# The opening of the first feed-forward: order of the first loads, scaling before squaring, and a norm factor computed with the tokens on partitions

## The chip, the core and the metric

The kernel runs on one core of a Trainium2 chip. The metric is the device time of one execution in microseconds (us), from the first to the last instruction of the program and what lies around it. Engines are named as in the profile: PE is TensorE, PEld its weight loads, DVE is VectorE, ACT is ScalarE, POOL is GpSimd and SP is SyncE, which here only issues DMAs.

## What is computed

One step of a decoder layer on 520 tokens: 512 of a new sequence and 8 of running sequences. The model width is 1024.

```
h = x
h = h + 0.5 * swiglu(rms_norm(h, ffn1_norm), gate1, up1, down1)      # 1024 -> 2816 -> 1024
h = h + mixer(rms_norm(h, mix_norm), ...)                            # pooling heads and SSD heads
h = h + 0.5 * swiglu(rms_norm(h, ffn2_norm), gate2, up2, down2)
y = rms_norm(h, final_norm)

rms_norm(x, g) = x * rsqrt(mean(x*x) + 1e-6) * g
swiglu(x)      = (silu(x @ gate) * (x @ up)) @ down
```

The change concerns the first line of this: the first norm and the first units of the first feed-forward. All values are float32.

## The kernel before

**Layout.** Features lie on the 128 partitions and tokens along the free axis, so `h` is 8 slices of 128 x 520, and every matmul has a 128 x 128 block of weights against 260 tokens, one of the two halves of the 520. A slice of `x` is written straight into `h`; its first slice comes with the vectors (norm gains and so on) in one DMA of 640 columns.

**Exact products from fast ones.** A matmul of plain float32 operands is two passes in the trace. Most products use three matmuls in the faster type fp32r instead (`mm3`): both operands are split into a rounded high part and a low part. `split` (L109 to L117) makes them for weights: ACT casts the high part (`whi`, `shi`), DVE or a POOL DMA that accumulates makes the low part (`wlo`, `slo`). `prep_pair` (L217) makes `xth` and `xtl` from the scaled input `xg` in the same way.

**The norm factor is applied late.** The kernel multiplies with `xg = x * gain` (`scaled`, L213), and the factor `r = 1/sqrt(mean + eps)` of each token is multiplied into the products when they leave PSUM (`plain_out`, L390 onwards). So `r` is not needed before the first unit is complete. `squares` (L163, L166) has ACT square the slices and DVE add them into `acc`. In `scales`, the 128 partitions of `acc` are summed by two matmuls with a matrix of ones (`psr_f`, L173), which leaves the sum of each token on all 128 partitions; ACT takes the root (L174, after a load of its function table) and DVE the reciprocal (L175) of 128 x 260 values, twice.

**The opening.** A unit is 128 of the 2816 hidden features, with a gate block and an up block. Unit 0 is multiplied in plain float32 while the input is still arriving (`plain`, L340): for each j of 0 to 3, slices j and j + 4 of `x` are loaded, then the two parts of the gate and up block (`raw`) that belong to them. The second unit, number 3, is partly plain (L360) and partly split (L369, `plain_mixed`, with `pwhi` and `pwlo` made by ACT and POOL). The third unit, number 1, is the first with the full split scheme (tiles `whi_1a`, `shi_1c`, `shi_1d`, `whi_1b` and their low parts).

**PSUM.** Eight banks in four tags of two. Tag `ps` serves, in turn, the sums of the norm (`psr`), and the up block of unit 3 (`P_310`, `P_311`). A third tile under that tag has to wait until the first has been read.

**Order.** A scheduler orders each engine's instructions at build time from its own estimate of their times. `tc.high_priority()` lets a block go ahead, and `tc.issue_after(i)` puts instructions of the same engine behind `i`. Each engine is given its instructions as one list and works it off in that order. SP issues all the loads of weights and input, in the written order; the eight loads in flight use eight semaphores in turn.

The second feed-forward has the other way of making the factor already, in `turned_scales` (L525): the sums are made with the tokens on 104 partitions, 5 groups of them (`turned`, L186: five matmuls with `acc` as weights and two columns of ones), so that root and reciprocal work on 104 x 10 values, and then five matmuls with an identity matrix `ident` (`spread`, L197) put the result on all 128 partitions again, in two PSUM tiles `pr_t` of tag `ps`, from which ACT copies it to `r` (L531).

Of the kernel before, what the change touches and what calls it, by code (L numbers as in the profile page):

```python
# [23 lines left out]
KD = D // P  # L24
# [38 lines left out]
def tile_trunk_step(ctx: ExitStack, tc: tile.TileContext, ins: dict, outs: dict):  # L63
    nc = tc.nc
# [23 lines left out]
    ident = cst.tile([P, P], F32, tag="ident", name="ident")  # L88
# [3 lines left out]
    def raw_pair(name, hp=None):  # L92
        hp, nb = (wp, 2) if hp is None else (hp, 1)
        return hp.tile([P, 2, 1024], F32, tag="raw", bufs=nb, name=f"raw_{name}")
# [66 lines left out]
    def squares(nx, wx, d, name, hp=("tg", 2)):  # L161
        if d == 0:
            nc.scalar.activation(out=nx[2], in_=h[:, d], func=AF.Square)  # L163
            return
        sq = wx.tile([P, 2, HB], F32, tag=hp[0], bufs=hp[1], name=f"sq_{name}_{d}").rearrange("p b t -> p (b t)")
        made = nc.scalar.activation(out=sq, in_=h[:, d], func=AF.Square)  # L166
        nc.vector.tensor_tensor(out=nx[2], in0=nx[2], in1=sq, op=ALU.add)
        return made.ins
# [39 lines left out]
    def home(gp, nb, name):  # L208
        return gp.tile([P, 4, HB], F32, tag="g", bufs=nb, name=name)

    def scaled(xg, norm, j):
        for d, out in ((j, xg[:, 0::3]), (j + KD // 2, xg[:, 1:3])):
            nc.scalar.activation(out=out, in_=h[:, d].rearrange("p (b t) -> p b t", b=2), func=AF.Copy,  # L213
                                 scale=v(norm, d))
        return xg

    def prep_pair(nx, xg, xd, j):  # L217
        xth, xtl, _, _ = nx
        nc.vector.tensor_tensor(out=xd[:, 0:2], in0=xg[:, 0::2], in1=xg[:, 3:4].to_broadcast([P, 2, HB]),
                                op=ALU.subtract)  # L220
        nc.vector.scalar_tensor_tensor(out=xd[:, 2], in0=xd[:, 1], scalar=-1.0, in1=xg[:, 0], op0=ALU.mult,
                                       op1=ALU.subtract)
        nc.vector.scalar_tensor_tensor(out=xd[:, 3], in0=xd[:, 2], scalar=-1.0, in1=xg[:, 1], op0=ALU.mult,
                                       op1=ALU.subtract)
        for s, t in ((xg[:, 0:3], slice(0, 3)), (xd, slice(3, 7))):
            nc.scalar.copy(xth[:, j, t], s)
            nc.vector.tensor_tensor(out=xtl[:, j, t], in0=s, in1=xth[:, j, t].bitcast(F32), op=ALU.subtract)

    class Ffn:
# [81 lines left out]
                low(go, slice(1, 3))  # L311
                low(xd, slice(3, 7))

        def plain_load(self, f, j=None):
            if f not in self.raw:
                self.raw[f] = raw_pair(f"{self.i}_{f}")
            src = ins[f"w{self.i}gu"]
            for u in range(2):
                if j is None:
                    nc.sync.dma_start(out=self.raw[f][:, u], in_=src[2 * f + u])  # L320
                    continue
                q = (t.rearrange("p (q c) -> p q c", q=2)[:, :, j * P : j * P + P]
                     for t in (self.raw[f][:, u], src[2 * f + u]))
                nc.sync.dma_start(out=next(q), in_=next(q))
# [349 lines left out]
    ffn1 = Ffn(nx1, 1, wx1, None, 2)  # L674
    xg1 = []
    second = ffn1.order[1]
    for j in range(KD // 2):
        for d in (j, j + KD // 2):
            q = slice(NVEC + d * NT if d else 0, NVEC + (d + 1) * NT)
            nc.sync.dma_start(out=vx[:, q], in_=ins["x"][:, q])  # L680
        ffn1.plain_load(0, j)
        xg1.append(scaled(home(xo, 8, f"xg_f1{j}"), "ffn1_norm", j))
        with tc.high_priority():
            for d in (j, j + KD // 2):
                last = squares(nx1, wx1, d, "f1", ("ac", 3) if j == KD // 2 - 1 else ("tg", 2))
        ffn1.plain(0, xg1[j], j)
        prep_pair(nx1, xg1[j], home(xo, 8, f"xd_f1{j}"), j)
# [1 line left out]
    third = ffn1.order[2]  # L689
    ffn1.early[third] = ffn1.fetch(f"1_{third}", ins["w1gu"][2 * third : 2 * third + 2], xo)  # L690
    with tc.high_priority():
        root = ffn1.scales()
    ffn1.add_early(third)
    with tc.issue_after(last):
        ffn1.plain_split(second, xo)
# [48 lines left out]

    ps[0] = tc.alloc_tile_pool(name="ppm", bufs=8, space=PSUM, reuse_waits="tile")
    mixer(tc, ins, outs, dict(locals()))
    f2["xg"].release()
    xa[0].release()
# [5 lines left out]
    with tc.high_priority():  # L754
        f2["ffn"].plain_free(0)
        root = f2["ffn"].turned_scales()
# [63 lines left out]
def mixer(tc, ins, outs, e):  # L820
    nc = tc.nc
# [8 lines left out]
    mp = pool("mx", "right")  # L830

    ident = e["ident"]
    nc.sync.dma_start(out=ident, in_=ins["ident"])
    tri = cst.tile([P, P], F32, tag="tri", name="tri")
    nc.sync.dma_start(out=tri, in_=ins["tri"])
    sel = cst.tile([48, NH], F32, tag="sel", name="sel")
# [575 lines left out]
```

## Time and profile before

| | |
|---|---|
| time, median of 3 runs | 966.94 us (966.36 to 967.24) |
| the profiled execution | 964.7 us, of which the span of the trace is 962.9 us |
| PE / DVE / ACT / POOL busy | 941.1 / 857.9 / 693.7 / 231.2 us |
| share of the chain that ended last | PE 80%, DVE 9%, DMA 4%, ACT 3% |
| granted TensorE clock, mean | 0.996 |

The profiled execution is 2.2 us under the median, and 1.8 us of it lie outside the trace's span. Times in the profile count from the span's start. The chain of waits is followed back from the last instruction, so a step that is not in it can move by some amount with no effect. Matmuls overlap: a row's duration covers the pipeline too, and the distance from start to start says what a matmul costs.

### The profile page before, as it was taken

What the parts mean: (1) busy time and instruction counts of PE and PEld (TensorE: products, weight loads), DVE (VectorE), ACT (ScalarE), POOL (GpSimd) and SP (SyncE); (2) the same over time, 40 slices, a digit from 0 to 9 for tenths busy, and PEclk for the clock granted to TensorE, in tenths of its full rate; (3) what the DMA queues carried; (4) which work ended last, traced back from release to release, by engine and by line L of the source; (5) the groups of instructions that cost most, each with busy time, mean ns of one, the idle gap of its engine ahead of it and who ended that gap; (6) DMA issues with size and microseconds to landing.
All of it is one profiled execution on the core that took longest, in us unless ns stands there. A gap on an engine that the chain in (4) does not pass through costs nothing.

```text
span 962.9 us, 20257 instructions
## 1 busy us (share of the span) xinstructions
PE 941.1 (98%) x7652; PEld 922.7 (96%) x7652; DVE 857.9 (89%) x1613; ACT 693.7 (72%) x1296; POOL 231.2 (24%) x341
## 2 busy tenths in 40 slices
PE   7999999999999999999999999999999999999995
PEld 6999999999999999999999999999999999999995
DVE  7999899989989698688999966899999999999976
ACT  8777677667776475586758556777788878887964
POOL 0111211221121000156523111022243324332500
PEclk9999999999999999999999999999999999999998
DMA  8575775675657343246698777457598769877832
GB/s 245 149 174 118 181 178 129 151 187 135 164 140 173 84 151 110 61 165 179 160 270 224 162 176 166 115 140 177 129 226 218 160 165 223 191 166 173 215 102 90
DMA packets 66611, 157.01 MB, mean 163 GB/s; under 512 B 9480, under 2 KB 22728, under 8 KB 66512
## 3 DMA queue, kind: packets, MB, share of 16 engines
q1 hardware_dynamic: 41040, 103.78, 34.3%
q0 software_dynamic: 25472, 51.92, 29.8%
q8 instruction: 60, 0.98, 0.4%
q14 instruction: 39, 0.32, 0.1%
HBM read 148.33 MB, written 7.34 MB: 162 GB/s over the span
## 4 chain that ended last, share of the span: by engine, by line
PE 80%; DVE 9%; DMA 4%; ACT 3%; issue 2%; POOL 2%; DVEq 0%; SPq 0%; ACTq 0%; POOLq 0%
PE A L130 8%; PE A L126 8%; PE A L129 8%; PE BE L130 6%; PE BE L129 6%; PE BE L126 6%; PE P L340 3%; PE wo L126 2%; PE wo L130 2%; PE wo L129 2%; PE A2d L129 2%; PE A2d L126 2%; PE A2d L130 2%; PE A1d L130 2%; PE A1d L129 2%
## 5 line engine op out<-in xcount | busy, mean ns | idle before, releaser
L482 ACT COPY ac<-A 128x260 f32<-128x260 f32 x123 | 45.4, 369 | 13.5 <-PE A L130 13.5
L425 DVE TENSOR_TENSOR s<-raw 128x1024 f32<-128x1024 f32 x41 | 50.0, 1220 | 3.4 <-DMA raw<-in_w1gu 2.5
L126 PE MATMUL wo<-catg,whi_wo 128*128 128x260 f32 x128 | 37.2, 291 | 0.0
L340 PE MATMUL P<-xg_f,raw 128*128 128x260 f32 x128 | 31.8, 400 | 5.5 <-ACT sq_f L166 5.5
L126 PE MATMUL inz<-xh_mx,whi_inz 128*128 128x260 f32 x128 | 36.7, 287 | 0.0
L130 PE MATMUL inz<-xh_mx,wlo_inz 128*128 128x260 f32 x128 | 36.3, 284 | 0.3 <-DMA wlo_inz<-in_w_in 0.3
L126 PE MATMUL inx<-xh_mx,whi_inx 128*128 128x260 f32 x128 | 36.4, 284 | 0.0
L130 PE MATMUL wo<-catg,wlo_wo 128*128 128x260 f32 x128 | 36.2, 283 | 0.0
L129 PE MATMUL inz<-xl_mx,whi_inz 128*128 128x260 f32 x128 | 36.1, 282 | 0.0
L130 PE MATMUL inx<-xh_mx,wlo_inx 128*128 128x260 f32 x128 | 36.1, 282 | 0.0
L129 PE MATMUL wo<-catg,whi_wo 128*128 128x260 f32 x128 | 36.1, 282 | 0.0
L129 PE MATMUL inx<-xl_mx,whi_inx 128*128 128x260 f32 x128 | 36.1, 282 | 0.0
L1091 POOL DMA_DIRECT2D out_nss<-hs x32 | 20.5, 640 | 59.9 <-DVE hs L1109 58.8
L340 PEld LDWEIGHTS P<-xg_f,raw 128*128 128x128 f32 x128 | 25.0, 200 | 9.3 <-ACT sq_f L166 5.5
L1222 DVE TENSOR_TENSOR h<-wo,h 128x260 f32<-128x260 f32 x48 | 19.4, 422 | 14.8 <-PE wo L130 14.8
L950 DVE SCALAR_TENSOR_TENSOR A<-U,h,A 128x544 f32<-128x544 f32 x36 | 28.1, 782 | 4.3 <-ACT A L948 4.0
L494 DVE TENSOR_TENSOR tg<-BE,ac 128x520 f32<-128x520 f32 x41 | 28.5, 695 | 2.2 <-PE BE L130 2.1
L504 DVE TENSOR_TENSOR tg<-tg,r_f 128x520 f32<-128x520 f32 x41 | 28.6, 698 | 1.5 <-ACT tg L502 1.2
L109 ACT CAST whi_wo<-raw_wo 128x1024 fp32r<-128x1024 f32 x12 | 12.6, 1047 | 22.7 <-issue 18.2
L502 ACT ACTIVATE tg<-tg 128x520 f32<-128x520 f32 x41 | 26.2, 639 | 3.5 <-DVE tg L501 3.5
L501 DVE TENSOR_TENSOR tg<-tg,r_f 128x520 f32<-128x520 f32 x41 | 28.5, 696 | 0.1
L426 DVE TENSOR_TENSOR s<-s,raw 128x512 f32<-128x512 f32 x41 | 28.2, 688 | 0.0
(1812 smaller groups left out, 4805.3 us busy)
## 6 DMA issues: line engine op xcount, KB each, us to landing
raw<-in_w2gu SPq DMA_DIRECT2D x44, 512.0 KB, 4.8
raw<-in_w1gu SPq DMA_DIRECT2D x42, 512.0 KB, 4.7
raw_1d<-in_w1d SPq DMA_DIRECT2D x24, 384.0 KB, 3.6
raw_2d<-in_w2d SPq DMA_DIRECT2D x24, 384.0 KB, 4.1
raw_wo<-in_w_out SPq DMA_DIRECT2D x12, 512.0 KB, 5.2
wlo_wo<-in_w_out POOLq DMA_DIRECT2D x12, 512.0 KB, 6.9
ab<-scr_acs SPq DMA_DIRECT2D x8, 512.0 KB, 5.5
raw_inz<-in_w_in SPq DMA_DIRECT2D x8, 512.0 KB, 4.4
```

The source lines that it names most:

```text
L126: first = nc.tensor.matmul(ps, whi, xhi, start=start, stop=False, **kw)
L129: nc.tensor.matmul(ps, whi, xlo, start=False, stop=False, **kw)
L130: nc.tensor.matmul(ps, wlo, xhi, start=False, stop=stop, **kw)
L340: nc.tensor.matmul(self.banks[f, u][b][:, :HB], ws(self.raw[f][:, u], j + 4 * q), xg[:, slot[q]], start=j == q == 0, stop=j == 3 and q == ...
L425: nc.vector.tensor_tensor(out=s1, in0=diag, in1=up0, op=ALU.add)
L426: nc.vector.tensor_tensor(out=s2[:, 0], in0=s1[:, 1], in1=raw[:, 0, :nb], op=ALU.add)
L482: nc.scalar.copy(keep, out[:, :HB])
L494: nc.vector.tensor_tensor(out=tg, in0=self.BE[k][:, :, :HB], in1=a, op=ALU.add)
L501: nc.vector.tensor_tensor(out=tg, in0=tg, in1=r, op=ALU.mult)
L502: nc.scalar.activation(out=tg, in_=tg, func=AF.Silu)
L504: nc.vector.tensor_tensor(out=tg, in0=tg, in1=r, op=ALU.mult)
L950: nc.vector.scalar_tensor_tensor(out=A[:, :n], in0=U[:, j : j + n], scalar=w(j), in1=A[:, :n], op0=ALU.mult, op1=ALU.add)
```

## The change

Three edits in the opening of the first feed-forward, and a DMA that moves with them.

1. `plain_load` takes the block (`u`) that it loads; the loop issues slice j, the gate part, slice j + 4, the up part, where it issued both slices first and then both parts.
2. For j = 0 the squares lose their high priority, so that the scaling of the slice (`scaled`) goes first.
3. `ffn1.scales()` becomes `ffn1.turned_scales()`. The value it returns, behind which the splits of the third unit are put by `issue_after(root)`, is now the reciprocal on DVE and no longer the root on ACT.
4. `ident`, which the new way needs, is loaded at j = 1 by SP, ahead of slices 2, 6, 3 and 7 of `x`; before it stood with the mixer's constants.

```
-        def plain_load(self, f, j=None):
+        def plain_load(self, f, j=None, us=(0, 1)):
...
-            for u in range(2):
+            for u in us:
...
     for j in range(KD // 2):
-        for d in (j, j + KD // 2):
+        for u, d in enumerate((j, j + KD // 2)):
             q = slice(NVEC + d * NT if d else 0, NVEC + (d + 1) * NT)
             nc.sync.dma_start(out=vx[:, q], in_=ins["x"][:, q])
-        ffn1.plain_load(0, j)
+            ffn1.plain_load(0, j, (u,))
+        if j == 1:
+            nc.sync.dma_start(out=ident, in_=ins["ident"])
         xg1.append(scaled(home(xo, 8, f"xg_f1{j}"), "ffn1_norm", j))
-        with tc.high_priority():
+        with tc.high_priority() if j else nullcontext():
             for d in (j, j + KD // 2):
                 last = squares(nx1, wx1, d, "f1", ("ac", 3) if j == KD // 2 - 1 else ("tg", 2))
...
     with tc.high_priority():
-        root = ffn1.scales()
+        root = ffn1.turned_scales()
     ffn1.add_early(third)
...
     with tc.issue_after(root):
         ffn1.open(third)
...
-    nc.sync.dma_start(out=ident, in_=ins["ident"])
```

What the scheduler makes of it, at three places. On SP, the first loads before (`h` is the input, `raw_0` the blocks of unit 0):

```order
L680 DMA h<-in_x 128x640
L680 DMA h<-in_x 128x520
L324 DMA raw_0_93<-in_w1gu 128x2x128 x2
L680 DMA h<-in_x 128x520 x2
L324 DMA raw_0_93<-in_w1gu 128x2x128 x2
```

and now:

```order
L680 DMA h<-in_x 128x640
L324 DMA raw_0_92<-in_w1gu 128x2x128
L680 DMA h<-in_x 128x520
L324 DMA raw_0_92<-in_w1gu 128x2x128
L680 DMA h<-in_x 128x520
L324 DMA raw_0_92<-in_w1gu 128x2x128
L680 DMA h<-in_x 128x520
L324 DMA raw_0_92<-in_w1gu 128x2x128
L683 DMA ident<-in_ident 128x128
```

The first gate part is now second in the queue and no longer third, and `ident` goes ahead of four slices of the input.

On ACT, from the last preparation of unit 3's weights (`pwlo_31`) to the root of the norm, before:

```order
L349 ACTIVATE pwlo_31_233<-raw_3_208 128x1024
L226 CAST xth_f_87<-xd_f_171 128x1040
L226 CAST xth_f_87<-xg_f_183 128x780
L226 CAST xth_f_87<-xd_f_200 128x1040
L174 ACT_TABLE_LOAD
L174 ACTIVATE r_f_90<-psr_f_214,eps 128x260
L174 ACTIVATE r_f_90<-psr_f_218,eps 128x260
L109 CAST whi_1a<-raw_1_211 128x1024
L113 ACTIVATE wlo_1a<-raw_1_211 128x512
L109 CAST shi_1c<-s_1_1_222 128x1024
```

and now:

```order
L349 ACTIVATE pwlo_31_244<-raw_3_209 128x1024
L109 CAST whi_1a<-raw_1_212 128x1024
L113 ACTIVATE wlo_1a<-raw_1_212 128x512
L226 CAST xth_f_87<-xg_f_184 128x780
L226 CAST xth_f_87<-xd_f_172 128x1040
L109 CAST shi_1c<-s_1_1_233 128x1024
L226 CAST xth_f_87<-xd_f_201 128x1040
L109 CAST shi_1d<-s_1_1_234 128x1024
L109 CAST whi_1b<-raw_1_212 128x512
L113 ACTIVATE wlo_1b<-raw_1_212 128x512
L194 ACT_TABLE_LOAD
L194 ACTIVATE rt_t<-psr_t,eps 104x10
```

All six splits of the third unit (`1a` to `1b`) moved from behind the root to ahead of its table load.

On PE, in the second unit, before (`pwhi` and `pwlo` are the high and low parts of its weights):

```order
L369 MATMUL P_301_238<-xth_f_87,pwhi_30_227 128x260
L360 MATMUL P_311_240<-xg_f_96,raw_3_208 128x260
L360 MATMUL P_311_240<-xg_f_125,raw_3_208 128x260
L360 MATMUL P_311_240<-xg_f_154,raw_3_208 128x260
L360 MATMUL P_311_240<-xg_f_183,raw_3_208 128x260
L369 MATMUL P_300_237<-xtl_f_88,pwhi_30_227 128x260
```

and now:

```order
L369 MATMUL P_300_248<-xth_f_87,pwlo_30_239 128x260 x2
L369 MATMUL P_301_249<-xth_f_87,pwlo_30_239 128x260
L200 MATMUL pr_t_224<-ident,rt_t 128x104 x3
L200 MATMUL pr_t_229<-ident,rt_t 128x104 x2
L360 MATMUL P_311_251<-xg_f_96,raw_3_209 128x260
L360 MATMUL P_311_251<-xg_f_126,raw_3_209 128x260
L360 MATMUL P_311_251<-xg_f_155,raw_3_209 128x260
L360 MATMUL P_311_251<-xg_f_184,raw_3_209 128x260
```

The gate block of unit 3 is now finished first (36 matmuls of L369, `pwhi` and `pwlo`), then come the five matmuls of `spread`, and all of the up block (`P_311`, `P_310`) stands behind them, because its PSUM tiles follow those of the norm factor in tag `ps`.

## The prediction

> **What bounds the kernel now.** I read the page first (busy times, then the shares of the chain that ended last), then the busy times by stretch, then the opening row by row.
>
> ```profile
> PE 941.1 (98%) x7652; PEld 922.7 (96%) x7652; DVE 857.9 (89%) x1613; ACT 693.7 (72%) x1296; POOL 231.2 (24%) x341
> PE 80%; DVE 9%; DMA 4%; ACT 3%; issue 2%; POOL 2%; DVEq 0%; SPq 0%; ACTq 0%; POOLq 0%
> 10.00:20.00 10.00, 10.00 (x48) 8.66 (x47) 9.73 (x16) 10.00 (x15) 0.15 (x1) 1.00 0.90 299
> 20.00:30.00 10.00, 10.00 (x63) 9.21 (x62) 9.84 (x12) 9.97 (x14) 2.61 (x3) 1.00 0.86 210
> ```
>
> The last two rows give, for a stretch of 10 us, the busy time of PE, PEld, DVE, ACT and POOL. PE is the bound of the whole program: what starts PE earlier is won, what makes it wait is lost, and what another engine saves is worth only what PE waited for it. In the stage that is changed, ACT is as full as PE (10.00 and 9.97 of 10 from 10 to 30 us). ACT's 72% is an average that hides this; whatever is queued on ACT there and needed by PE has no slack.
>
> **The start.** The timeline of the first microseconds, and how long the loads of the two lines take to land:
>
> ```profile
> 0.74 0.88 SPq L680 DMA_DIRECT2D h<-in_x  x2
> 1.67 1.32 SPq L324 DMA_DIRECT2D raw<-in_w1gu  x2
> 3.67 0.64 ACT L163 ACTIVATE acc_f<-h 128x520 f32<-128x520 f32 x1 [1.64 <-DMA h<-in_x]
> 4.21 0.71 ACT L213 ACTIVATE xg_f<-h 128x520 f32<-128x520 f32 x1
> 5.51 12.61 PE L340 MATMUL P<-xg_f,raw 128*128 128x260 f32 x48 [5.51 <-ACT sq_f L166]
> DMA to landing us min/median/max: 3.4/3.8/4.6
> ```
>
> The profile puts PE's first wait down to a square on ACT, but the first matmul reads only `xg` and `raw`. `xg` is there at 4.21 + 0.71 = 4.92; the first part of the weights, issued at 1.67, lands at 1.67 + 3.8 = 5.5 by the median of L324 (last row). So the weights end this wait. After the change, the weights are issued behind one slice and not two, 0.44 earlier (half of 0.88), and `xg` starts at 3.67 and ends at 4.38, since the square no longer precedes it. PE can then start between 4.4 (weights no longer late, 1.1 saved) and 5.5 (landing unchanged). I take 0.7 saved, between the 0.44 of the issue and the 1.1 of ACT. The second part of the weights and slice 4 land about where they did, the queue holding the same bytes; PE needs them four passes later, and is then at half pace (below), so no wait follows.
>
> **The root on ACT.** These rows are ACT's work right behind the last `xth` cast, in order; the six splits of the third unit are the rows from `whi_1a` to `wlo_1b`:
>
> ```profile
> 24.09 1.28 ACT L174 ACT_TABLE_LOAD   x1
> 25.38 0.85 ACT L174 ACTIVATE r_f<-psr_f,eps 128x260 f32<-128x260 f32 x2
> 26.12 1.04 ACT L109 CAST whi_1a<-raw 128x1024 fp32r<-128x1024 f32 x1
> ...
> 29.99 0.63 ACT L113 ACTIVATE wlo_1b<-raw 128x512 fp32r<-128x512 f32 x1
> 30.64 1.28 ACT L392 ACT_TABLE_LOAD   x1
> ```
>
> The six take from 26.12 to 30.64, 4.52 us. In the new order they stand ahead of the table load, because `issue_after` now names an instruction of DVE and no longer holds ACT's. ACT is unbroken up to there in both, and starts at 3.67 in both (the landing of slice 0 is unchanged), so the load moves from 24.09 to 24.09 + 4.52 = 28.6. The costs of the steps that follow are in the second feed-forward, which has the same ones:
>
> ```profile
> L191 PE MATMUL psr_t<-ones,acc_f x10: 168/231/231, 618.7 to 619.5; 128*104 128x2 f32 x10
> L194 ACT ACTIVATE rt_t<-psr_t,eps x1: 270/270/270, 619.7 to 619.7; 104x10 f32<-104x10 f32 x1
> L195 DVE RECIPROCAL rt_t<-rt_t x1: 207/207/207, 620.8 to 620.8; 104x10 f32<-104x10 f32 x1
> L531 ACT COPY r_f<-pr_t x2: 338/378/419, 624.1 to 624.5; 128x312 f32<-128x312 f32 x1, 128x208 f32<-128x208 f32 x1
> 623.40 1.10 PE pr_t L200 x10
> ```
>
> 28.6 + 1.29 (table load) + 0.27 (root) + 0.21 (reciprocal) = 30.4: from then on `spread` can run.
>
> The Trainium skill ("ScalarE: Activation LUTs", What ACT_TABLE_LOAD costs) counts about 2.66 us for a switch of the table, of which 1.38 are a drain. Here the load and all that goes with it last from 24.09 to 25.38, 1.29; by the skill's figure the root, and with it the time, would come some 1.4 later still. The trace has the very same switch, and I use it.
>
> **When PE comes to `spread`.** The chain of waits in order of time has PE's path through this stage:
>
> ```profile
> 22.51 0.88 PE psr_f L173 x4
> 24.26 2.39 PE P L369 x20
> 26.65 1.75 PE P L360 x8
> 28.41 6.25 PE P L369 x52
> 34.65 0.12 PE BE L126
> ```
>
> The sums cost the same in either way: 0.88 for the four passes of `psr_f`, and 10 passes of `psr_t` from 618.7 to 619.5. So the first L369 would start at 24.26 - 0.7 = 23.6. A matmul of L369 costs (2.39 + 6.25) / 72 = 0.12 us. Ahead of `spread` stand 36 of them, 4.3 us: PE is there at 27.9 and **waits 2.5 us**, to 30.4. The wait cannot be passed by: everything behind `spread` is the up block, whose PSUM tiles become free only when ACT has copied `pr_t`. Then: `spread` 1.1 (ten passes, all new on PE); 0.1 for the end of ACT's first copy (0.42), mostly beside the second group; 1.75 of L360; the other 36 of L369, 4.3. Sum: 30.4 + 1.1 + 0.1 + 1.75 + 4.3 = 37.65 where it was 34.65, **3.0 later**. As terms: -0.7 start, +2.5 wait, +1.1 `spread`, +0.1 copy. The first two hang together: the root comes when ACT comes to it, so a start that wins more makes the wait longer by as much.
>
> **DVE and what comes after.** DVE loses two reciprocals of 3.41 together and gets one of 0.21. PE is worth this only where it waited for DVE:
>
> ```profile
> 26.37 3.41 DVE L175 RECIPROCAL r_f<-r_f 128x260 f32<-128x260 f32 x2
> 48.22 0.28 PE L129 MATMUL BE<-xtl_f,shi_4d 128*128 128x260 f32 x1
> 48.84 0.39 PE L130 MATMUL A<-xth_f,slo_4d 128*128 128x260 f32 x1 [0.34 <-DVE slo_4d L117]
> 90.00:100.00 10.00, 10.00 (x85) 10.00 (x84) 9.60 (x19) 6.13 (x12) 2.29 (x3) 1.00 0.74 162
> PE BE2d L126 <- ACT shi_2d_0c L109: 0.9, 1, 0.9
> ```
>
> At 48.84 PE starts 0.62 after the matmul before it and not 0.12: 0.5 of waiting for DVE. With PE 3.0 later and 3.2 less work on DVE it goes: **-0.5**. On the other side the scheduler's orders of ACT and DVE differ up to about 100 us, around the first down products, and DVE is nearly full there (9.60 of 10). A wait of this kind stands at the same place of the second feed-forward, 0.9 (last row). It can come, in full, or not: 0 to 0.9, and I take **+0.6**, as the new order of ACT puts other casts ahead of `shi_1d` there. After that the orders of all engines are the same to the end.
>
> The moved `ident` delays the four slices behind it by about its issue:
>
> ```profile
> 12.40 0.48 SPq L833 DMA_DIRECT2D ident<-in_ident  x1
> ```
>
> ACT is the only one to wait for slices, and from 10 us on it is unbroken, so it waits for none of these four now: I count nothing. If that cover is gone, ACT and with it the root are late by up to 0.5.
>
> **Sum.** -0.7 + 2.5 + 1.1 + 0.1 - 0.5 + 0.6 = +3.1. The profiled span of 962.9 becomes 966.0, its execution 967.8 from 964.7. The median of the runs is 2.2 over that execution; the same step on it gives 966.94 + 3.1 = **970.0 us**.
>
> **The rivals.**
>
> *Not slower: what is lost is given back.* PE's later waits could take the delay up, where what they wait for does not itself follow from PE. In the first feed-forward these are:
>
> ```profile
> PE A1d L130 <- DVE slo_1d_1d L117: 0.6, 1, 0.6
> PE dn L126 <- ACT gt L270: 0.6, 1, 0.6
> PE dn L129 <- DVE gt L271: 0.3, 1, 0.3
> PE dn L126 <- DVE h L611: 0.3, 1, 0.3
> ```
>
> Together 1.8. If all are paced by DVE work that runs ahead of PE, and the new wait does not come, 3.1 - 0.6 - 1.8 = 0.7 is left: 967.6. It decides from 1.2 given back on, where the total falls under 0.2% (1.93 us), about what a measurement of this kernel can tell from no change. Against it: all four are released by ACT or DVE, which work on what PE produced just before, so they shift with PE. 0.13.
>
> *No wait at all.* Were the root to run as soon as the sums are there, PE would pay only `spread`: -0.7 + 1.1 + 0.1 - 0.5 = 0: 966.9. Even the best start (1.1) gives 966.5, so this edit has no way to be faster by over 0.2% that I can price. Against it: the six splits stand ahead of the root on ACT, which is full. 0.05.
>
> *The clock falls back.* PE would idle for longer than anywhere in the trace.
>
> ```profile
> PE yd L1187 <- DVE zs L1211: 1.1, 1, 1.1
> PEclk9999999999999999999999999999999999999998
> 5.50:9.20 3.70, 3.69 (x9) 2.93 (x10) 3.34 (x6) 3.28 (x6) 0.00 (x0) 1.00 1.01 315
> 9.20:13.00 3.80, 3.80 (x19) 3.30 (x18) 3.80 (x8) 3.80 (x6) 0.00 (x0) 1.00 1.04 326
> ```
>
> The longest wait after the start is 1.1, and the clock row keeps its nines. But PE is slow at first: 9 passes in 3.70 us, then 19 in 3.80. If 2.5 idle brings such a stretch back, half of 3.7 is lost, 1.9: 971.9. The Trainium skill ("TensorE: Matmul & The Clock Gate", HAM oscillation) warns of idle gaps over some 3.4 us; by that rule a gap of 2.5 passes. No run yet shows it. 0.07.
>
> **How the numbers follow.** The forecast has the rest, 0.75. Its own ends: the new wait at 0 or 0.9 (-0.6, +0.3), the wait at 48.84 kept (+0.5), 0.3 either way on ACT's arrival at the root, 0.4 for the spread of runs: 968.7 to 971.5. The range takes in the clock at its upper end and part of what is given back at its lower: 968.2 to 972.0. Faster by over 0.2%: 0.03, out of the second rival's best end and what I don't see. Within 0.2%: the first two rivals' rest, 0.15. Slower: 0.82.
>
> **What would show it.** Right: PE's first matmul near 4.8; the table load of L194 near 28.6; a wait of PE before L200 of 2 to 3 us, put down to DVE's reciprocal; the first `A` or `BE` product of the third unit near 37.6; no wait at 48 to 52. Wrong: L194 close behind `psr_t`, or no wait at L200; PE's lead over the old trace shrinking between 100 and 340 us.

## Result and profile after

The changed kernel takes 970.85 us (median of 7 runs, 968.60 to 972.85) against 965.84 beside it (median of 7): a ratio of 1.0052, 95% interval 1.0038 to 1.0067. In two later series, each beside the kernel before, it was 971.05 (1.0063, 1.0049 to 1.0076) and 971.40 (1.0062, 1.0049 to 1.0075). The forecast was 970.0, within 968.2 to 972.0, and slower: that came true. The sum under it gave +3.1, and the runs give 5 to 5.9. The profiled execution after takes 970.2 with a span of 968.4, against 964.7 and 962.9 before.

The page of the changed kernel, busy times and shares of the chain:

```profile
PE 943.9 (97%) x7668; PEld 924.9 (96%) x7668; DVE 854.8 (88%) x1612; ACT 694.1 (72%) x1297; POOL 230.8 (24%) x341
PE 85%; DVE 5%; ACT 5%; DMA 3%; issue 1%; POOL 0%; SPq 0%; DVEq 0%; ACTq 0%; POOLq 0%
```

DVE has 3.1 us less to do and PE 2.8 more, and PE is still the bound. The timeline of the start (start, duration, engine, line; in brackets the idle time before it and what ended it):

```profile
1.20 0.69 SPq L324 DMA_DIRECT2D raw<-in_w1gu  x1
1.94 0.58 SPq L680 DMA_DIRECT2D h<-in_x  x1
3.83 0.73 ACT L213 ACTIVATE xg_f<-h 128x520 f32<-128x520 f32 x1 [1.81 <-DMA h<-in_x]
5.15 1.64 PE L340 MATMUL P<-xg_f,raw 128*128 128x260 f32 x3 [5.15 <-ACT acc_f L163]
5.87 0.73 ACT L213 ACTIVATE xg_f<-h 128x520 f32<-128x520 f32 x1 [0.78 <-DMA h<-in_x]
```

PE starts 0.36 earlier than in the first profile of before. ACT does not: its first slice is there 0.16 later, and it waits 0.78 for slice 4, which is now issued behind a load of weights (0.42 for a slice before). The chain of waits, in order of time, through the norm factor to the third unit (its first product is a matmul into a PSUM tile `A` or `BE`):

```profile
29.03 1.28 ACT L194
...
30.32 0.28 ACT rt_t L194
...
30.63 0.23 DVE rt_t L195
...
30.90 0.93 PE pr_t L200 x6
...
31.85 0.43 ACT r_f L531
...
32.32 2.02 PE P L360 x8
34.34 4.32 PE P L369 x36
38.66 0.12 PE A L126
```

Before, this chain ran on PE alone. Now it leaves PE, goes over ACT's table load, root, DVE's reciprocal, back to PE, once more to ACT for the copy, and the third unit begins at 38.66 instead of 34.65. PE's waits, by releaser (total, times, longest):

```profile
PE pr_t L200 <- DVE rt_t L195: 1.6, 1, 1.6
PE inz L130 <- DMA wlo_inz<-in_w_in: 1.4, 1, 1.4
PE BE1d L126 <- ACT shi_1d_0c L109: 0.9, 1, 0.9
```

The first is the forecast wait; the third is the possible new one near 95 us, which came in full. The second, for the low part of weights that the mixer loads (`wlo_inz`), was 0.3 in the first profile of before.

### The profile page after: what moved, and what is told of

The parts are those of the page before. It is cut to its first block, busy times and chain, and to the rows that moved or that the text cites. A ratio compares the mean times of both kernels' runs of the same rounds, so it can differ in the third digit from the quotient of the medians.

```text
span 968.4 us, 20284 instructions
## 1 busy us (share of the span) xinstructions
PE 943.9 (97%) x7668; PEld 924.9 (96%) x7668; DVE 854.8 (88%) x1612; ACT 694.1 (72%) x1297; POOL 230.8 (24%) x341
## 4 chain that ended last, share of the span: by engine, by line
PE 85%; DVE 5%; ACT 5%; DMA 3%; issue 1%; POOL 0%; SPq 0%; DVEq 0%; ACTq 0%; POOLq 0%
PE A L126 8%; PE A L130 8%; PE A L129 8%; PE BE L130 6%; PE BE L129 6%; PE BE L126 6%; PE wo L126 2%; PE wo L130 2%; PE wo L129 2%; PE A2d L129 2%; PE A2d L126 2%; PE A2d L130 2%; PE A1d L126 2%; PE A1d L130 2%; PE A1d L129 2%; PE P L340 1%
## 5 line engine op out<-in xcount | busy, mean ns | idle before, releaser
L130 PE MATMUL inz<-xh_mx,wlo_inz 128*128 128x260 f32 x128 | 36.3, 284 | 1.4 <-DMA wlo_inz<-in_w_in 1.4
L130 PE MATMUL wo<-catg,wlo_wo 128*128 128x260 f32 x128 | 36.2, 283 | 0.0
L130 PE MATMUL inx<-xh_mx,wlo_inx 128*128 128x260 f32 x128 | 36.2, 283 | 0.0
```

What stands on the lines that cost most here:

```text
L130: nc.tensor.matmul(ps, wlo, xhi, start=False, stop=stop, **kw)
```

## Experiments

All runs, with places in their profiles (us from the start of the span): PE's first matmul, the first matmul of `spread`, and the first product of the third unit (start of the matmul).

| kernel | median us (runs) | ratio to before, 95% | first matmul | first L200 | third unit |
|---|---|---|---|---|---|
| before, first profile | 965.84 (7) | 1 | 5.51 | | 34.49 |
| before, second profile | 966.36 (1) | | 5.78 | | 35.81 |
| before, third profile | 964.70 (1) | | 5.69 | | 34.95 |
| changed, first | 970.85 (7) | 1.0038 to 1.0067 | 5.15 | 30.90 | 38.49 |
| changed, second | 971.05 (6) | 1.0049 to 1.0076 | 4.78 | 30.75 | 39.69 |
| changed, third | 971.40 (5) | 1.0049 to 1.0075 | 4.58 | 30.96 | 38.56 |
| root ahead of the splits | 969.99 (5) | 1.0030 to 1.0055 | 4.87 | 29.20 | 37.94 |
| loads and scaling only | 966.53 (11) | 0.9995 to 1.0012 | 4.78 | | 34.00 |
| norm factor only | 970.19 (5) | 1.0034 to 1.0061 | 5.82 | 30.68 | 38.28 |
| before, PE warmed up | 967.52 (11) | 1.0005 to 1.0023 | 5.25 | | 33.33 |
| root ahead, copies on DVE | 968.38 (5) | 1.0020 to 1.0045 | 4.76 | 28.64 | 36.21 |
| the same, no square root | 967.85 (12) | 1.0014 to 1.0033 | 4.72 | 26.93 | 36.03 |
| changed, wait filled | 970.21 (6) | 1.0032 to 1.0057 | 4.75 | 30.98 | 38.56 |
| changed, wait longer | 972.91 (5) | 1.0063 to 1.0088 | 4.60 | 32.37 | 42.26 |

### The root ahead of the six splits

```diff
-        nc.scalar.activation(out=rt, in_=ps[:n, : 2 * m], func=AF.Sqrt, bias=eps[:n], scale=1.0 / D)
-        return rt, nc.vector.reciprocal(out=rt, in_=rt).ins
+        root = nc.scalar.activation(out=rt, in_=ps[:n, : 2 * m], func=AF.Sqrt, bias=eps[:n], scale=1.0 / D)
+        return rt, nc.vector.reciprocal(out=rt, in_=rt).ins, root.ins
...
-            return last
+            return root if self.i == 1 else last
```

> The changed kernel with one edit: what holds the six splits of the third unit back names the root on ACT again, not the reciprocal on DVE, so the root stands ahead of the splits. Theory (the splits ahead of the root make PE wait): the table load of L194 comes near 24.5 instead of 29.03, PE's wait of 1.6 before L200 goes, the copies of L531 fall behind the splits at about 29.5 and are free when spread ends near 30; the first product of the third unit comes near 37.0 instead of 38.7, and the time is 1.6 below the changed kernel, 3 to 3.5 above the kernel before. Rival (the way itself costs: ten more passes, two copies on ACT that PE waits for): the wait only moves from L200 to L360 or to the copies, and the time stays within 0.5 of the changed kernel, 4.5 to 5 above the kernel before.

PE's waits and ACT's timeline of this kernel:

```profile
PE P L360 <- ACT r_f L531: 1.3, 1, 1.3
```

```profile
25.44 1.28 ACT L194 ACT_TABLE_LOAD   x1
26.74 0.27 ACT L194 ACTIVATE rt_t<-psr_t,eps 104x10 f32<-104x10 f32 x1
...
30.78 0.63 ACT L113 ACTIVATE wlo_1b<-raw 128x512 fp32r<-128x512 f32 x1
31.31 0.64 ACT L531 COPY r_f<-pr_t 128x312 f32<-128x312 f32 x2
```

The root comes 3.6 earlier and the wait before L200 is gone, but the copies of L531 stand behind the last split now, and PE waits 1.3 before L360. The rival was right on the wait; the time lies between the two, 3.95 above the kernel before. The norm factor uses ACT twice, and PE waits for whichever of the two stands behind the splits.

### The loads and the scaling alone

The kernel before with `plain_load(0, j, (u,))` between the slices and the scaling ahead of the squares, and the old `scales()`.

> The kernel before with only the first two edits: the loads interleaved and the scaling ahead of the squares; the norm factor in the old way. Theory (the start is worth 0.4, and what it makes depends on when the clock becomes full): PE's first matmul near 5.1 instead of 5.5, and the time between 0.4 below the kernel before and 0.7 above it, by where the full clock comes (9.3 or 11.0 us from the span's start). Rival (the interleaved loads or the order on ACT make PE wait later in the opening): waits in the first 24 us that the kernel before does not have, and 1 or more above it.

No difference that these runs can tell. PE starts 0.7 to 1.0 earlier than in the three profiles of before and the third unit at 34.00; but then PE waits for DVE in a place where it did not before:

```profile
36.09 0.39 PE L126 MATMUL A<-xth_f,whi_1a 128*128 128x260 f32 x1 [0.48 <-DVE tg L390]
```

At the product with `slo_4d` it is at 49.10, against 48.84, 49.31 and 50.16. From the third unit to there it takes 15.10, and 14.35 in each profile of before: 0.75 of the lead is lost on the way, 0.48 of it in this wait for DVE. This is one profile.

### The norm factor alone

The kernel before with `turned_scales()` and the earlier `ident`; the loads in the old order.

> The kernel before with only the norm factor in the new way, its loads in the old order. Theory (all of the loss is the norm factor's order on ACT, its ten passes and the wait near 95): table load of L194 near 28.6 to 29, PE's wait before L200 1.8 to 2.5, the first product of the third unit near 38, no wait at 48.84, a wait of 0.9 near 95; 3.5 to 4.5 above the kernel before. Rival (the first two edits bring the loss through a later full clock): 2 or less above it.

4.15 above the kernel before: the edit of the norm factor makes most of the loss, as the theory had it, and the first two edits alone cost nothing that the runs tell. The changed kernel lies 5.0 to 5.9 above before, so 0.9 to 1.7 come only with both. PE waits 1.6 before L200 here, and 1.6, 1.9 and 2.6 in the changed kernel; what a longer wait does to the clock is told below, but no run shows that this is the whole difference. The table load stands at 28.82, close to the 28.6 of the forecast, though ACT's first slice is there at 3.90 and not at 3.67.

### PE warmed up ahead of the first product

```diff
+    for k in range(2):
+        idle = bank(f"warm{k}")
+        for _ in range(4):
+            nc.tensor.matmul(idle[:, :P], ones, ones, start=True, stop=True)
```

> The kernel before with eight matmuls of ones by ones (128x128, float32) into two banks that nobody reads, ahead of the first product. Theory (PE runs at half pace until it has been busy for some 4 to 6 us, whatever it works on): the clock is full by 5 to 8 us from the span's start instead of 9.27, and the time is 0.7 to 1.9 below the kernel before. Rival (the clock follows the amount of work that counts, or a fixed time from the program's start): full near 9.3 all the same, and the time within 0.5 of the kernel before.

The windows of this kernel (PE's busy time and count of passes come first):

```profile
5.25:7.12 1.87, 1.86 (x5) 1.49 (x5) 1.33 (x3) 1.50 (x4) 0.00 (x0) 1.00 1.01 339
7.12:11.00 3.88, 3.88 (x19) 3.38 (x18) 3.88 (x7) 3.77 (x6) 0.00 (x0) 1.00 0.97 291
```

From 7.12 on there are 19 passes in 3.88 us; before, that pace came at 9.27. So the dummies did warm the clock in this profile, and the third unit came at 33.33. The time is 1.5 above before all the same: the scheduler ordered other rows of ACT and DVE anew for it, and PE now waits for ACT's copies five times between 36 and 97 us:

```profile
PE A L126 <- ACT ac L482: 0.9, 3, 0.4
PE A1d L126 <- ACT ac1d L482: 0.9, 2, 0.5
```

By `slo_1d_1d` (180.46, against 179.69 to 181.47) the lead is gone. Whether the new order or the lead itself brings these waits is not separated. The theory was right on the clock and wrong on the time.

### Root ahead, and the copies on DVE

The kernel with the root ahead of the splits, and:

```diff
-                nc.scalar.copy(r[:, q], spread(rt, n, js, f"t{b}")[:, : n * len(js)])
+                (nc.vector.tensor_copy if self.i == 1 else nc.scalar.copy)(r[:, q], spread(rt, n, js, f"t{b}")[:, : n * len(js)])
```

> The run with the root ahead of the splits showed the wait not gone but moved: 1.3 before L360, for ACT's copies of L531, which now stand behind the six splits. Here those two copies of the first feed-forward are DVE's, which has nothing queued there. Theory (PE waits for whatever of the norm factor stands behind the splits on ACT): no wait before L200 nor before L360; from the first pass of spread to the first product of the third unit 7.5 instead of 8.8; the time 1.3 below the run with the root ahead, about 968.7, and 2.6 above the kernel before: 1.1 of spread, 1.0 of the wait near 95, 0.5 of other things. Rival (the passes of spread themselves, or their bank of PSUM, hold PE): still 1 or more between the last pass of spread and L360, and the time as it was, about 970.

PE's timeline:

```profile
28.64 1.26 PE L200 MATMUL pr_t<-ident,rt_t 104*128 104x104 f32 x10
30.03 2.02 PE L360 MATMUL P<-xg_f,raw 128*128 128x260 f32 x8
```

No wait before either, and 7.57 from the first pass of `spread` to the third unit, as the theory said. Against the kernel before of its own series it is 3.05 above, where the kernel with the root ahead was 3.95 above and the changed one beside it 5.72. So what stood behind the splits on ACT is about half of the loss, the half clock that the wait brings (below) included: all six runs of the changed kernel in that series have a mean clock of 0.995 or less; the step from the root alone to root and copies is 0.9 by the medians and 1.7 by the third unit of the two profiles, where 1.3 was expected.

### The same without the square root

```diff
+        if bare:
+            nc.vector.tensor_scalar(out=rt, in0=ps[:n, : 2 * m], scalar1=1.0 / D, scalar2=EPS, op0=ALU.mult, op1=ALU.add)
+            last = nc.vector.reciprocal(out=rt, in_=rt).ins
+            return rt, last, last
```

> As the run with the copies on DVE, and in the first feed-forward the square root is left out: the mean of the squares plus eps on DVE, then its reciprocal, so that ACT has neither the root nor its table load there (the output is not the reference's). It gives a bound for the edit: the norm factor in the new way with nothing of it on ACT. Theory (what remains is PE's own): no wait before L200 or L360, 1.1 of spread and at most 1.0 near 95 remain, less the 1.3 and 0.3 that ACT no longer does; the time 966 to 968, 0 to 2 above the kernel before. Rival (the loss is the first two edits' start, or the way of the norm factor on PE): no better than the run with the copies on DVE.

967.85, inside the expected range, and still 2.5 above before (0.14% to 0.33%). With nothing of the norm factor on ACT, the ten passes of `spread`, 1.03 on PE (26.93 to 27.96), and three waits for ACT's copies between 76 and 98 us, 1.3 together, remain. The rival is not excluded: 967.85 is 0.5 below the run with the copies on DVE, and the runs of the two overlap. No form of this way that was tried beats the kernel before.

### The changed kernel and the kernel before once more

> The changed kernel once more, for the profile of another execution. Theory (ACT's queue, not PE's start, sets when spread can run): the full clock comes at another time from the span's start, and PE's wait before L200 is the longer the earlier it comes (1.6 at 10.99; about 2.5 at 9), while the first L200 stays between 30.6 and 31.0 and the first product of the third unit near 38.5. Rival (PE's late arrival sets it): the wait stays 1.6 and the third unit moves with the clock. The median stays between 969.5 and 971.5.

> The kernel before once more, for the profile of another execution: its first one was 964.7, below the median of 966. Theory (part of the difference between the two profiles is not the change's): the wait for wlo_inz, 0.3 in the first profile and 0.8 to 1.4 in all five kernels run since, is 0.8 to 1.4 here too, and the execution is nearer to 966. Rival (the change makes that wait): it is 0.3 again. By the clock: here the full clock moves the third unit, since no wait stands between.

The first pass of `spread` stands at 30.75 to 30.96 in all three profiles of the changed kernel, while PE's first matmul moves from 5.15 to 4.58 and the wait from 1.6 over 1.9 to 2.6: ACT's queue sets the time, and an earlier PE only waits longer. In the kernel before the third unit follows the clock. Its windows up to and behind the step of pace, first and second profile:

```profile
5.51:9.27 3.76, 3.76 (x9) 2.99 (x10) 3.40 (x6) 3.34 (x6) 0.00 (x0) 1.00 1.01 315
9.27:13.00 3.73, 3.73 (x19) 3.23 (x18) 3.73 (x8) 3.73 (x6) 0.00 (x0) 1.00 1.04 325
```

```profile
5.78:11.66 5.88, 5.88 (x14) 4.64 (x15) 4.79 (x9) 4.72 (x8) 0.00 (x0) 1.00 1.00 329
11.66:15.00 3.34, 3.34 (x17) 2.90 (x16) 3.34 (x6) 3.34 (x7) 0.00 (x0) 1.00 0.98 325
```

Half pace lasts 3.76 us in one and 5.88 in the other, and the third unit comes at 34.49 and 35.81. (The clock column, third from the end, reads 1.00 there; the count of passes tells it.) The profile on which the forecast was made had the earliest third unit of the three.

The surprise is in the second profile of the changed kernel. Its windows around `spread`:

```profile
27.53:30.94 3.41, 1.50 (x12) 1.29 (x12) 0.82 (x2) 2.88 (x5) 0.85 (x1) 1.00 1.01 279
30.94:34.36 3.42, 3.42 (x14) 3.13 (x14) 1.67 (x4) 1.67 (x3) 0.00 (x0) 0.50 0.72 196
34.36:37.77 3.41, 3.41 (x26) 3.26 (x25) 3.41 (x6) 1.64 (x3) 0.00 (x0) 1.00 0.33 92
```

PE is busy for 1.50 of 3.41 us, and for the next 3.42 the granted clock is 0.50. The third unit begins at 39.69 and not at 38.5. This is the third rival of the prediction.

### Wait filled, wait longer

```diff
+            if self.i == 1:
+                idle = bank("fill")
+                for _ in range(14):
+                    nc.tensor.matmul(idle[:, :P], ident, ident, start=True, stop=True, skip_group_check=True)
```

> The second execution of the changed kernel showed a stretch of half clock from 30.9 to 34.4, right behind PE's wait for the root; the first one did not. Here 14 matmuls of ident by ident (128x128, float32, some 1.5 us) into a bank that nobody reads stand on PE between the sums and the first L369; all other engines' orders are the same, row for row. Theory (the clock falls back when too much of one of its windows of 3.41 us is idle): PE's wait before L200 shrinks to some 0.2 to 0.6, the first L200 stays at 30.6 to 31.0, no half clock follows it in any run (no mean clock below 0.996), and the median is 969.5 to 970.3, about 1 below the changed kernel, with a narrower scatter. Rival (the fall is chance, or costs nothing): the time stays with the changed kernel's 971, or is above it by the added work.

```diff
+        for _ in range(times):
             nc.scalar.activation(out=rt, in_=ps[:n, : 2 * m], func=AF.Sqrt, bias=eps[:n], scale=1.0 / D)
...
-            rt, last = turned([acc], n, "t")
+            rt, last = turned([acc], n, "t", 5 if self.i == 1 else 1)
```

> The changed kernel with the square root on ACT done five times over in the first feed-forward (the same result), 4 x 0.27 = 1.1 more ahead of the reciprocal; nothing else moves. Theory (idle time in one window brings the half clock): PE's wait before L200 is 2.7 to 3.2, the half clock follows in every run (mean clock 0.995 or less in all), and the time is 1.1 plus part of 1.7 above the changed kernel, 972 to 973.5. Rival (only the wait counts): 1.1 above it, with the mean clocks as they are there.

> The changed kernel beside the two, on the same chip. Theory: its runs fall into two groups by the mean clock, 0.996 and more near 970, 0.995 and less near 972; a profile with PE idle for over 2 us of one window of 3.41 has the half clock behind it, one with less has not. Rival: no such grouping.

The windows of the kernel with the longer wait, and of the third profile of the changed kernel:

```profile
27.48:30.90 3.42, 1.35 (x12) 1.14 (x10) 1.07 (x1) 3.36 (x6) 0.85 (x1) 1.00 0.95 238
30.90:34.31 3.41, 1.94 (x9) 1.95 (x10) 0.22 (x1) 1.36 (x5) 0.00 (x0) 0.50 0.90 264
34.31:37.72 3.41, 3.41 (x11) 2.73 (x11) 3.25 (x6) 2.38 (x4) 0.00 (x0) 0.50 0.00 1
```

```profile
26.77:30.18 3.41, 1.63 (x14) 1.42 (x12) 1.24 (x1) 3.39 (x5) 0.81 (x1) 1.00 1.03 280
30.18:33.59 3.41, 2.56 (x16) 2.25 (x17) 1.44 (x5) 2.10 (x5) 0.04 (x1) 1.00 1.01 261
```

With the longer wait two windows in a row are at half clock (the first of them has 1.47 idle), all five runs have a mean clock of 0.994, and the time is 1.5 above the changed kernel's beside it. In the third profile of the changed kernel PE waits longer (2.6) than in the second (1.9), yet the clock holds: the wait lies across the edge of two windows, 1.78 idle in one and 0.85 in the next. In the first profile the most that one window had was 1.61:

```profile
28.05:31.47 3.42, 1.81 (x16) 1.61 (x15) 0.45 (x2) 2.51 (x4) 0.86 (x1) 1.00 1.03 319
```

With the wait filled (the dummies took 3.2 us, not the 1.5 expected), PE has none left before L200, L200 stands at 30.98 as ever, the profile has no half clock behind `spread`, and none of six runs has a mean clock below 0.996. The median is 1.2 below the changed kernel's beside it, though the runs overlap. Its profile has a half clock elsewhere, in the mixer, behind a wait of 2.2 for a load:

```profile
523.95:527.37 3.42, 1.29 (x10) 1.29 (x11) 3.25 (x19) 3.39 (x8) 0.88 (x1) 1.00 0.50 94
527.37:530.78 3.41, 3.41 (x18) 3.41 (x17) 3.38 (x15) 1.71 (x3) 1.94 (x2) 0.50 0.90 182
```

Over all 18 runs of the changed kernel, 12 have a mean clock of 0.995 or less and take 971.8 in the mean, 6 have 0.996 or more and take 970.2. Half of 3.41 us is 1.7; the groups differ by 1.6. Of 50 runs of the kernel before in the later series none is below 0.996, nor is any of the kernels with the copies on DVE; with the root ahead it is one of five, and with the norm factor alone, where PE starts later, none of five. The mean clock is a rough sign for a single run. One window at half lowers the mean of a span of 968 by 0.0018, and the clock also falls after the last matmul, where it costs nothing; by where that falls, the eleven profiles without a half clock in between read 0.996 or 0.997. So 0.995 or less points to such a half clock, but 0.996 does not exclude one: the filled kernel's profile has 0.996. The groups cross, too (970.21 with 0.995, 971.40 with 0.996). That the share is zero on one side and two thirds on the other is not changed by this. So the idle window is shown as the cause of the half clock, by filling it and by lengthening it.

### Before, a third profile

> A third profile of the kernel before. Its first two have a wait of 0.3 and 0.5 for wlo_inz in the mixer, the profiles of the ten other executions (the changed kernel's and the experiments') 0.8 to 2.2, though the orders there are the same. Theory (scatter of a load): 0.8 or more in this one. Rival (the kernels that were changed in the opening load later there): 0.3 to 0.5 again. By the clock: the first product of the third unit comes 25.4 after the full clock sets in at 9.3, 24.3 after it at 11.7; 34.6 to 36 here.

```profile
PE inz L130 <- DMA wlo_inz<-in_w_in: 0.5, 1, 0.5
```

0.3, 0.5 and 0.5 in before, 0.8 to 2.2 in all the other profiles: the rival was right in that it goes with the kernel. But the one with PE warmed up has the old loads and still waits 1.2 there, so a changed opening load is not the reason. What it is stays open.

## Why the prediction was right, and where it was not

Starts of matmuls in the profiles; of the changed kernel, the two profiles without a half clock behind `spread` (first and third). `slo_4d` and `slo_1d_1d` are low parts of weights, the first of a later unit, the second of a down product; `dn` are later down products of the first feed-forward, `wo` the mixer's output products.

| place | before (three) | changed (two) | later by, means | forecast |
|---|---|---|---|---|
| first matmul | 5.51, 5.78, 5.69 | 5.15, 4.58 | -0.8 | -0.7 |
| third unit's first product | 34.49, 35.81, 34.95 | 38.49, 38.56 | +3.4 | +3.0 |
| `A` with `slo_4d`, L130 | 48.84, 50.16, 49.31 | 51.87, 51.93 | +2.5 | +2.5 |
| `A1d` with `slo_1d_1d` | 179.69, 181.48, 179.92 | 183.97, 184.01 | +3.6 | +3.1 |
| first `dn` | 326.36, 327.33, 326.61 | 330.75, 329.86 | +3.5 | +3.1 |
| first `wo` | 529.30, 531.47, 529.65 | 535.26, 534.01 | +4.5 | +3.1 |
| span | 962.9, 964.6, 962.9 | 968.4, 967.9 | +4.7 | +3.1 |

- **The start** (-0.7): right in size, -0.8. As the prediction said, it has no worth with the wait behind it.
- **The wait at L200** (+2.5): its cause was right in each link: splits ahead of the root, ACT late, PE waiting, the reciprocal as releaser. The wait itself was 1.6, 1.9 and 2.6, by when the clock became full. The start of `spread` was forecast at 30.4 and is 30.75 to 30.96. The step that is off is "ACT starts at 3.67 in both": in the first profile it starts at 3.83 and waits 0.78 for slice 4, and the table load comes at 29.03, not 28.6. Most of that is scatter and not the change. In the other two profiles of before the old table load stands later than the 24.09 of the first:

```profile
24.90 1.28 ACT L174 ACT_TABLE_LOAD   x1
24.71 1.28 ACT L174 ACT_TABLE_LOAD   x1
```

With the 4.52 of the six splits the three give 28.6, 29.4 and 29.2; the changed kernel has 29.03, 28.88 and 29.09.
- **`spread` and the copy** (+1.1 and +0.1): by the chain of waits it took 1.42 from the first pass to L360 in place of 1.2, and the eight passes of L360 2.02 in place of 1.75.
- **The wait at 48.84** (-0.5): gone, and 0.4 more with it up to that place.
- **The new wait near 95** (+0.6, between 0 and 0.9): came in full. On ACT the cast waits for a product of PE first, as in the second feed-forward (`94.64`, idle 1.74); PE goes back and forth with ACT there:

```profile
94.64 0.83 ACT L109 CAST shi_1d_0c<-s_1d 128x768 fp32r<-128x768 f32 x1 [1.74 <-PE A1d L129]
```

- **"After that the orders are the same to the end"**: true of the orders, not of the time. Between the first `dn` and `wo` another 1.0 comes, part of it the wait for `wlo_inz`. From the first `dn` to the first `wo` the changed kernel takes 204.5 and 204.2, before 202.9, 204.1 and 203.0; so one of the three profiles of before is as long. This is open.
- **Rival, given back** (0.13): did not come. The lag does not shrink from 180 to 530 us.
- **Rival, no wait at all** (0.05): did not come; the table load stands behind the splits.
- **Rival, the clock falls back** (0.07, 971.9): by the mean clock it came in two runs of three, and such runs take 971.8. Its size was right and its chance was not. I had asked for 2.5 idle to bring it, against 1.1 as the longest seen; the runs show that 1.9 idle inside one window of 3.41 is enough, and that the 1.8 of another is not. The Trainium skill ("TensorE: Matmul & The Clock Gate", HAM oscillation) speaks of idle gaps over some 3.4 us; here the half clock followed waits of 1.9 and 2.2, and the measurement decides.
- **The base**: the median of before given at first, 966.94 of three runs, lies above the 965.3 to 966.0 of the later series, and the profile had the earliest third unit of three. The forecast of 970.0 was therefore nearer to the result than its sum of +3.1, by luck.

Put together from the profiles: 2.3 for the two waits on ACT (third unit 38.5, against 36.2 with root and copies out of the way), 1.1 for the rest of the new way up to there (36.2 against 35.1, `spread` above all), 0.9 given back by 48 us, 1.1 near 95, 1.0 in the mixer: 4.6 of the 4.7 by which the spans differ. In two runs of three the clock adds 1.6, 1.1 in the mean; together 5.8, where the three medians are 5.0, 5.7 and 5.9 above before. Of the 2.7 by which the sum of +3.1 is short of this, 1.1 is the clock, which it left to a rival, 1.0 the mixer, and 0.5 the stretch near 95.

## What to carry to other kernels

A step of an engine that runs ahead of the bound is cheap only where nothing of it is queued behind other work: here a norm factor with 0.21 us of reciprocals in place of 3.41 made the kernel 5 us slower, and about half of that because its root and its copies stood behind six splits on a full ACT. When an instruction that a scheduler holds others behind is moved to another engine, look at what the old one held back. And price a wait of the bound engine with the clock: where 1.9 us or more of one window of 3.41 were idle, the next one ran at half here.

## What the hardware showed that I had not expected

The stretches between two changes of the clock are multiples of 3.41 us in all 14 profiles (20.48 is 6 of them, 945.49 is 277), and where the first one falls differs from execution to execution: PE ran at half pace for 3.8 to 6.3 us after its first matmul. In all of them the full clock came at the end of the first window of 3.41 us, counted back from a change, that PE filled; in the warmed kernel of one with 0.41 idle; with the root ahead a window with 0.49 idle did not bring it. So the same kernel's third unit moved by 1.3 between profiles, 1.1 of it by the clock, before any wait. The window at half clock with 1.47 idle, which another one followed, agrees with this. The full clock ended behind windows in which PE was idle for 1.91, 2.07 and 2.13 us by the profile's ends of matmuls, which are modelled, and held behind windows with 1.61 and 1.78. This is no sharp bound: at the end of the program, where nothing is lost by it, it also ended behind one with 1.65 (before, first profile) and one with 1.73 (root ahead). The window of before's end, and the first two of the kernel with the root ahead:

```profile
951.35:954.77 3.42, 1.77 (x6) 0.59 (x4) 3.42 (x7) 1.87 (x5) 0.00 (x0) 1.00 0.48 162
```

```profile
4.38:7.79 3.41, 2.92 (x7) 2.02 (x8) 0.67 (x2) 2.11 (x5) 0.00 (x0) 1.00 0.91 294
7.79:11.20 3.41, 3.41 (x9) 2.70 (x8) 3.41 (x8) 3.41 (x6) 0.00 (x0) 1.00 0.99 304
```
